# A decoder layer on one core: gated columns moved ahead of the second latent columns, and 38 convolution taps shared by ScalarE and GpSimd

## The chip, the core and the metric

The kernel runs on one core of a Trainium2 chip. The time is the device time of one execution, in microseconds (us). The core's engines work side by side, each through a queue of its own in order: TensorE (PE in the profile; PEld is its weight load), VectorE (DVE), ScalarE (ACT), GpSimd (POOL) and SyncE (SP), which here issues nearly all DMAs. They wait for each other through semaphores.

## What is computed

One step of a one-layer decoder with two parallel groups, for a prompt of 512 rows and 64 sample rows (8 sequences of 8), cut from the reference:

```python
proj = h @ w_in                                   # h = rmsnorm(x): 1024 -> 384 + 256 + 32 + 2*512
cq, ckv, kr, glu_in = ...                         # the 672 latent columns, the 1024 gated ones
q = einsum('btc,chd->bthd', rmsnorm(cq, g_q_norm), w_uq)
kv_rows = concat([rmsnorm(ckv, g_kv_norm), rope(kr)])
glu = glu_in[..., :512] * sigmoid(glu_in[..., 512:])
o_lat = attention over kv_rows (prompt), over 2048 cached rows + kv_rows (sample)
y = causal depthwise conv of glu, width 31, + b_dw          # 31 taps for each of 512 channels
conv_y = silu(layernorm(y, g_ln, b_ln))
x = x + concat([rmsnorm(attn), rmsnorm(conv_y)]) @ w_o
x = x + gated MLP with a width-3 convolution              # 1024 -> 2*2816 -> 1024
```

## The kernel before

Rows are kept transposed: channels lie on the 128 partitions, the 512 prompt and 64 sample rows along the free axis. Every matmul is made three times, with each operand split in a high and a low part (`mm3`, `mm3x`); `split` makes the parts, ScalarE the high one (CAST, L110) and VectorE the low one (L111). The stages are:

1. Input norm, transposed into `hTh`/`hTl`.
2. `latent_cols(0)`: the first 336 latent columns, PSUM banks named `pq`.
3. `glu()`: a generator over four blocks m of 128 gated channels. A block is two steps, the sigmoid half first, each of 48 matmuls of 288 columns into two banks `gb`, with weights `wg` from `wload`. After the second, VectorE writes `gx[:, m]` (L291 to L293), the input of the convolution. Weight tiles, raw, high and low, have two buffers each, so the high part of a step can be cast only when the matmuls of the step two before are done. The five banks of the stage go round, so a bank that `gx` reads is wanted again three steps later.
4. `latent_cols(1)`: the other 336 latent columns, three chunks of weights `w`, 45, 45 and 30 matmuls.
5. `latent(i)`, `q_rows`, `sample_queries`: norms, rotary parts and queries. Each `latent(i)` has GpSimd compute a reciprocal root (`rstd_of`, L119).
6. Sample attention in slots J = 0 to 37, four to a sequence, over key chunks of 512 rows: transposes `ktb`, scores `sb`, probabilities `ptb`, values `ob`.
7. `conv_norm`: from slot `CN0` on, two half steps a slot: transposes of the convolution's result `acc` (`lnb`), its statistics, `lnt`, the silu.
8. Prompt attention, output projection, gated MLP (`up`, `down`): the 600 us behind.

The convolution needs 31 taps for each of the four blocks m; a tap multiplies 128x512 elements of `gx[:, m]`, shifted by k, by a column of weights and adds the product to `acc[:, m]`. VectorE does a tap in one instruction (L246, SCALAR_TENSOR_TENSOR); GpSimd needs two, a product into a tile `ct` of two buffers (L249, TENSOR_SCALAR) and a sum (L250, TENSOR_TENSOR). `conv_sample(m)` is the same for the sample rows, on VectorE: per half a product `cs` of 128x992 (L258) and a sum (L260).

Before, four GLU steps (`GL0`) come first: block 0 and block 1. VectorE does taps 0 to 19 of block 0, GpSimd the other 11 into `acc2`; then `latent_cols(1)`, one GLU step, and three more between the queries. GpSimd does all 31 taps of block 1 and, behind the last `latent`'s reciprocal root (`issue_after(last["pow"])`), all of block 3 and four of block 2; VectorE does 12 taps of block 2 ahead of the slots and 15 more, one a slot, between them (`later`). `conv_norm` starts in slot 21.

What sets the order: the kernel is written for a scheduler, which puts each engine's instructions in one fixed sequence by their dependences and a running priority. `with prio(key)` shifts that priority for a block (a positive number: later). On the chip each engine then takes its sequence in order.

Of the kernel before, what the change touches and what calls it, by code (L numbers as in the profile page):

```python
# [10 lines left out]
F32 = mybir.dt.float32  # L11
# [3 lines left out]
AF = mybir.ActivationFunctionType  # L15
ALU = mybir.AluOpType
# [3 lines left out]
P = 128  # L20
NP = 512
# [42 lines left out]
def hymba_step(ctx, tc, x, cache, pt, sconv, sffn, vec, rows, w1, wglu, wuq, wuk, wuv, wukT,  # L64
# [79 lines left out]

    # ------------------------------------------------------------------ pools, first loads
    PR = dict(p0=-20, pr=-30, fs=-60, expo=80, wv=140, ft=-40, f0=-600, v2=600, av=-75, cs0=600, cv=65, vs=-55, cn=-150, att=-80, cs1=600, l4=20, q0=305, later=80, h2=70, l1=50, sq0=-45, lo=-360, wk=80, vb=20, lT=-15, v0=40, gl2=70, wo=-540, g0=-600, rq=600, cso=600, gl1=-40, sc1=25, rr=80, keys=-35, k0=600, pn=15, fs0=-60, ho=-45)

# [34 lines left out]
    def vcol(key, i):  # L182
        a = VEC[key][0] + i
        return vc[:, a:a + 1]
# [23 lines left out]

    # ------------------------------------------------------------------ input norm
    hTh = ps0.tile([P, 8, NT], F32R, name="hTh")  # L210
    hTl = ps0.tile([P, 8, NT], F32R, name="hTl")
    for i, (t0, n) in enumerate(TILES):
# [6 lines left out]
        for g in range(2):  # L219
# [5 lines left out]

    # ------------------------------------------------------------------ GLU columns, depthwise convolution
    GP = CW - 1 + NP
# [6 lines left out]
           for k in range(8)]  # L234
    acc = pcv.tile([P, 4, NT], F32, name="acc", tag="acc")

    def conv_taps(m, ks, E, first, dst=None):
        am = acc[:, m, 0:NP] if dst is None else dst
        for j, k in enumerate(ks):
            w = vcol("wdw", m * CW + k)  # L240
            xm = gx[:, m, k:k + NP]
            if j == 0 and first:
                b = vcol("bdw", m) if dst is None else 1.0
                E.tensor_scalar(am, xm, w, b, ALU.mult, ALU.add if dst is None else ALU.mult)
            elif E is V:
                V.scalar_tensor_tensor(am, xm, w, am, ALU.mult, ALU.add)  # L246
            else:
                t = pql.tile([P, NP], F32, name="ct", tag="ct", bufs=2)
                G.tensor_scalar(t, xm, w, 1.0, ALU.mult, ALU.mult)  # L249
                G.tensor_tensor(am, am, t, ALU.add)  # L250

    def conv_sample(m, E):
# [10 lines left out]

    GL0 = 4
    NV0 = 20
    NV2 = 12
    NV3 = 0
    NG2 = 4
    NL = 1
    LA = 0  # L270
    LS = 2
    last["kl"] = {}
    acc2 = pcv.tile([P, NP], F32, name="acc2")

# [35 lines left out]
    pj.append(ps1.tile([P, 672], F32, name="pj4", tag="pj4"))  # L310
    def latent_cols(c, order):
        pb = [bank("pq") for _ in range(5)]
        for (k0, kn) in ((0, 3), (3, 3), (6, 2)):
            w = wload(wp, w1[c][:, k0 * 336:(k0 + kn) * 336], kn * 336, "w1")
            for i in order:
                t0, n = TILES[i]
                for k in range(kn):
                    sl = slice(k * 336, (k + 1) * 336)
                    mm3(pb[i][:n, :336], hTh[:, k0 + k, t0:t0 + n], hTl[:, k0 + k, t0:t0 + n],
                        w[0][:, sl], w[1][:, sl], k0 + k == 0, k0 + k == 7)  # L320
        for i in order:
            n = TILES[i][1]
            A.copy(pj[i][:n, c * 336:(c + 1) * 336], pb[i][:n, :336])
# [5 lines left out]
    gl = glu()  # L329
    for _ in range(GL0):  # L330
        next(gl)
    with prio("cs0"):
        conv_sample(0, V)
    with prio("v0"):
        conv_taps(0, range(NV0), V, True)
    with prio("g0"):
        conv_taps(0, range(NV0, CW), G, True, acc2)
    latent_cols(1, ORD)

# [113 lines left out]
    with prio("l4"):  # L453
        latent(4)
        split(krn[:DR, 0], krn[:DR, 1], krT[:, NP:NT])
    with prio("gl1"):
        next(gl)
    wq_ = [wload(wp, wuq[c], 1152, "wuq") for c in range(2)]
# [6 lines left out]
    for i in range(4):  # L465
# [10 lines left out]
        with prio("rq"):  # L476
            rope_rows(qv[:, :, DN:], qv[:, :, DN:], i, P, H, "rq")
    with prio("cs1"):
        conv_sample(1, V)
    with tc.issue_after(last["pow"]):  # L480
        conv_taps(1, range(CW), G, True)
    for _ in range(4):
        with prio("sq1"):
            next(sq_, None)
        with prio("gl2"):
            next(gl, None)
    for _ in gl:
        pass

# [6 lines left out]

    with prio("v2"):
        conv_taps(2, range(NV2), V, True)
    V.tensor_tensor(acc[:, 0, :NP], acc[:, 0, :NP], acc2, ALU.add)

    def wload_into(hi, lo, src):
# [3 lines left out]

    later = [(2, -1)] + [(2, k) for k in range(NV2, CW - NG2)] + [(3, -1)] + [(3, k) for k in range(CW - NV3, CW)]
    with tc.issue_after(last["pow"]):
        conv_taps(3, range(CW - NV3), G, True)
        if NG2:
            conv_taps(2, range(CW - NG2, CW), G, True, acc2)  # L510

    s1.close()

    # ------------------------------------------------------------------ sample attention
    use_banks(k="k", s="s", x="x", o="o", b="k")
# [12 lines left out]
    RAW = 2  # L528
    CN0 = 21
    page_dma = []  # L530
# [251 lines left out]

    # ------------------------------------------------------------------ prompt attention
    R = {}
# [16 lines left out]
    def open_left():  # L801
# [171 lines left out]

    # ------------------------------------------------------------------ order of work
    assert NV2 > 0 and len(later) <= NL * (CN0 - LS)
    for J in range(NCR):
# [7 lines left out]
    for J in range(NJ + 6):  # L984
        if J == NJ + 1:
            open_right()
        if J == CN0 and NG2:
            G.tensor_tensor(acc[:, 2, :NP], acc[:, 2, :NP], acc2, ALU.add)
        if J >= CN0:
# [6 lines left out]
        if J == 30:  # L996
            wv = pcv.tile([P, 2, 1024], F32R, name="wv", tag="gx")
            with prio("wv"):
                wload_into(wv[:, 0], wv[:, 1], wuv)
        for m, k in later[:NL if J >= LS else 0]:  # L1000
            later.pop(0)
            with prio("later"), tc.issue_after(last["kl"][J + LA]):
                if k < 0:
                    conv_sample(m, V)
                else:
                    conv_taps(m, [k], V, False)
        if J >= CN0:
# [352 lines left out]
```

## Time and profile before

| | |
|---|---|
| three runs | 921.27 us median, 921.2 to 922.46 |
| profiled execution: span from first to last instruction | 919.5 us |
| around the span, taken as median less span | 1.8 us |
| PE busy | 864.1 us, 94% |
| mean granted TensorE clock | 0.976 |
| chain that ended last | PE 72%, POOL 18%, DVE 5% |

The profile gives no time of the profiled execution beyond its span; the difference to the median is taken as the work around it. A row of a timeline reads: start, duration, engine, line, operation, what it writes and reads, tile shapes, the count of instructions that stand together, and in brackets the engine's idle time before it and what ended that. Line numbers in rows are those of the kernel before.

### The profile page before, as it was taken

How to read it: one execution, taken by the hardware profiler on the slowest of the kernel's cores; microseconds unless marked ns; L12 is line 12 of the kernel's file. 1: busy time of each engine (PE TensorE's matmuls, PEld its weight loads, DVE VectorE, ACT ScalarE, POOL GpSimd, SP SyncE). 2: the span in 40 equal slices, each digit the busy share in tenths (PEclk: the TensorE clock that was granted, in tenths of full speed). 3: DMA queues.
4: the chain of work that ended last, by engine and by line, in shares of the span. 5: the costliest groups of instructions: out<-in, count | busy, mean ns of one | idle time of the engine just before them, and what ended most of it. 6: DMA issues, size and time to landing. Idle time of an engine off the chain costs nothing.

```text
span 919.5 us, 15985 instructions
## 1 busy us (share of the span) xinstructions
PE 864.1 (94%) x5820; PEld 773.8 (84%) x5820; DVE 606.3 (66%) x1097; ACT 431.4 (47%) x1008; POOL 288.3 (31%) x378
## 2 busy tenths in 40 slices
PE   7997977799989999998989999999999999999995
PEld 5997867666667767876769999999999999999995
DVE  6289789899987677777675666673124667665333
ACT  6322633577758976455453334333223343333333
POOL 3076299999981110000111122110001112211222
PEclk9998989899999999999999999999999999999998
DMA  7222114454442014011233222222332223223212
GB/s 231 81 61 75 58 62 130 123 153 117 116 110 80 26 47 149 24 47 28 65 109 115 91 89 73 86 64 67 88 110 94 75 87 92 71 63 99 70 41 104
DMA packets 37651, 79.80 MB, mean 87 GB/s; under 512 B 4226, under 2 KB 21699, under 8 KB 37572
## 3 DMA queue, kind: packets, MB, share of 16 engines
q1 hardware_dynamic: 37282, 78.22, 28.2%
q8 instruction: 46, 0.75, 0.3%
q10 hardware_dynamic: 290, 0.56, 0.2%
q14 instruction: 33, 0.27, 0.1%
HBM read 74.78 MB, written 3.98 MB: 86 GB/s over the span
## 4 chain that ended last, share of the span: by engine, by line
PE 72%; POOL 18%; DVE 5%; issue 2%; ACT 2%; DMA 1%; POOLq 0%; DVEq 0%; ACTq 0%
PE ub L129 10%; PE ub L131 10%; PE ub L133 10%; POOL acc L250 10%; POOL ct L249 7%; PE db L133 5%; PE db L131 5%; PE db L129 5%; PE ob L651 2%; PE wob L123 2%; PE wob L125 2%; PE wob L124 2%; DVE acc L246 2%; PE pq L125 1%; PE pq L124 1%
## 5 line engine op out<-in xcount | busy, mean ns | idle before, releaser
L129 PE MATMUL ub<-h2h,wup_h 128*128 128x288 f32 x704 | 154.0, 296 | 0.0
L131 PE MATMUL ub<-h2l,wup_h 128*128 128x288 f32 x704 | 153.9, 295 | 0.0
L133 PE MATMUL ub<-h2h,wup_l 128*128 128x288 f32 x704 | 152.7, 294 | 0.0
L133 PEld LDWEIGHTS ub<-h2h,wup_l 128*128 128x128 f32 x704 | 114.4, 189 | 0.0
L129 PEld LDWEIGHTS ub<-h2h,wup_h 128*128 128x128 f32 x704 | 114.0, 189 | 0.2
L131 PEld LDWEIGHTS ub<-h2l,wup_h 128*128 128x128 f32 x704 | 114.2, 189 | 0.0
L111 DVE TENSOR_TENSOR wup_l<-wup_r,wup_h 128x1024 fp32r<-128x1024 f32 x44 | 53.9, 1225 | 84.0 <-ACT wup_h L110 84.0
L250 POOL TENSOR_TENSOR acc<-acc,ct 128x512 f32<-128x512 f32 x73 | 108.1, 1480 | 2.8
L1180 POOL COPY nf<-U 128x2 f32<-128x2 f32 x44 | 28.7, 652 | 216.5 <-ACT U L1178 216.5
L249 POOL TENSOR_SCALAR ct<-gx,vc 128x512 f32<-128x512 f32 x73 | 78.8, 1090 | 0.0
L119 POOL TENSOR_TENSOR rstd<-ms,mhalf 128x1 f32<-128x1 f32 (+3 forms) x25 | 17.1, 687 | 195.5 <-ACT junk L971 111.4
L131 PE MATMUL db<-gl,wdn_h 128*128 128x288 f32 x352 | 78.4, 297 | 0.0
L129 PE MATMUL db<-gh,wdn_h 128*128 128x288 f32 x352 | 78.1, 299 | 0.0
L133 PE MATMUL db<-gh,wdn_l 128*128 128x288 f32 x352 | 77.6, 297 | 0.0
L110 ACT CAST wup_h<-wup_r 128x1024 fp32r<-128x1024 f32 x44 | 46.2, 1051 | 41.3 <-PE ub L131 30.7
L111 DVE TENSOR_TENSOR wdn_l<-wdn_r,wdn_h 128x768 fp32r<-128x768 f32 (+1 forms) x32 | 28.4, 888 | 54.9 <-ACT wdn_h L110 54.9
L110 ACT CAST wdn_h<-wdn_r 128x768 fp32r<-128x768 f32 (+1 forms) x32 | 25.0, 781 | 74.7 <-PE db L131 64.2
L131 PEld LDWEIGHTS db<-gl,wdn_h 128*128 128x128 f32 x352 | 57.9, 190 | 0.0
L133 PEld LDWEIGHTS db<-gh,wdn_l 128*128 128x128 f32 x352 | 57.5, 190 | 0.0
L129 PEld LDWEIGHTS db<-gh,wdn_h 128*128 128x128 f32 x352 | 57.0, 189 | 0.0
L246 DVE SCALAR_TENSOR_TENSOR acc<-gx,vc,acc 128x512 f32<-128x512 f32 x45 | 54.2, 1204 | 0.8
L110 ACT CAST gh<-uo 128x512 fp32r<-128x512 f32 (+1 forms) x44 | 16.9, 431 | 77.8 <-DVE uo L1191 77.8
(352 smaller groups left out, 2096.6 us busy)
## 6 DMA issues: line engine op xcount, KB each, us to landing
wup_r<-in_wup_dram SPq DMA_DIRECT2D x44, 512.0 KB, 3.5
CR<-in_cache_dram SPq DMA_DIRECT2D x128, 144.0 KB, 2.2
wdn_r<-in_wdn_dram SPq DMA_DIRECT2D x16, 384.0 KB, 3.1
wdn_r<-in_wdn_dram SPq DMA_DIRECT2D x16, 320.0 KB, 2.9
x<-in_x_dram SPq DMA_DIRECT2D x8, 512.0 KB, 5.9
wg_r<-in_wglu_dram SPq DMA_DIRECT2D x8, 512.0 KB, 3.2
wo_r<-in_wo_dram SPq DMA_DIRECT2D x8, 512.0 KB, 3.5
out_y_dram<-x SPq DMA_DIRECT2D x4, 512.0 KB, 3.2
```

Of the source, the lines that this page charges most:

```text
L110: A.copy(hi, src)
L111: last["split"] = V.tensor_tensor(lo, src, f(hi), ALU.subtract).ins
L123: T.matmul(out, lh, rh, start=start, stop=False)
L124: T.matmul(out, lh, rl, start=False, stop=False)
L125: T.matmul(out, ll, rh, start=False, stop=stop)
L129: T.matmul(o, lh, rh, start=start, stop=False)
L131: T.matmul(o, lh, rl, start=False, stop=False)
L133: T.matmul(o, ll, rh, start=False, stop=stop)
L246: V.scalar_tensor_tensor(am, xm, w, am, ALU.mult, ALU.add)
L249: G.tensor_scalar(t, xm, w, 1.0, ALU.mult, ALU.mult)
L250: G.tensor_tensor(am, am, t, ALU.add)
L1180: G.tensor_copy(nf[:, ch, 0:2], u[:, NP:UP])
```

## The change

All eight GLU steps follow `latent_cols(0)` directly (`GL0 = 8`). Of block 0, VectorE takes taps 0 to 23; the other 7 and all 31 of block 1 are shared: ScalarE multiplies a shifted piece of `gx` by its weights (`A.activation` with `scale=w`) into `ct`, GpSimd adds it. These 38 are traced four after each GLU step from the third on and one after each row tile of `latent_cols(1)`, and are kept in that order on both engines. GpSimd does blocks 2 and 3 alone, 62 taps, behind the last latent's reciprocal root. The four `conv_sample` run in slots 4, 8, 12 and 16, and `conv_norm` starts in slot 23.

```diff
+    acc2 = ps1.tile([P, NP], F32, name="acc2")
+    def shared_taps():
+        for m, am, ks in ((0, acc2, range(NV0, CW)), (1, acc[:, 1, 0:NP], range(CW))):
+            for k in ks:
+                w = vcol("wdw", m * CW + k)
+                xm = gx[:, m, k:k + NP]
+                if k == ks[0]:
+                    b = vcol("bdw", m) if k == 0 else 0.0
+                    tc.keep_in_program_order(A.activation(am, xm, AF.Identity, scale=w, bias=b))
+                else:
+                    t = pql.tile([P, NP], F32, name="ct", tag="ct", bufs=2)
+                    tc.keep_in_program_order(A.activation(t, xm, AF.Copy, scale=w))
+                    tc.keep_in_program_order(G.tensor_tensor(am, am, t, ALU.add))
+                yield
-    GL0 = 4
-    NV0 = 20
-    NV2 = 12
...
+    GL0 = 8
+    NV0 = 24
...
-    for _ in range(GL0):
+    for t in range(GL0):
         next(gl)
-    with prio("cs0"):
-        conv_sample(0, V)
+        if t > 1:
+            taps(4)
     with prio("v0"):
-        conv_taps(0, range(NV0), V, True)
-    with prio("g0"):
-        conv_taps(0, range(NV0, CW), G, True, acc2)
-    latent_cols(1, ORD)
+        first_taps()
+    latent_cols(1, ORD, 1)
+    taps(2 * CW)
+    V.tensor_tensor(acc[:, 0, :NP], acc[:, 0, :NP], acc2, ALU.add)
...
-    with prio("cs1"):
-        conv_sample(1, V)
-    with tc.issue_after(last["pow"]):
-        conv_taps(1, range(CW), G, True)
...
-    with prio("v2"):
-        conv_taps(2, range(NV2), V, True)
...
     with tc.issue_after(last["pow"]):
-        conv_taps(3, range(CW - NV3), G, True)
-        if NG2:
-            conv_taps(2, range(CW - NG2, CW), G, True, acc2)
+        conv_taps(2, range(CW))
+        conv_taps(3, range(CW))
...
-    CN0 = 21
+    CN0 = 23
...
-        for m, k in later[:NL if J >= LS else 0]:
-            later.pop(0)
+        for m in [J // 4 - 1] if J % 4 == 0 and 4 <= J < 20 else ():
             with prio("later"), tc.issue_after(last["kl"][J + LA]):
-                if k < 0:
-                    conv_sample(m, V)
-                else:
-                    conv_taps(m, [k], V, False)
+                conv_sample(m, V)
```

What the scheduler makes of it. VectorE in the gated stage, from the fourth weight split on; L245 and L247 are VectorE's taps now, L318 to L320 write `gx`. Of the change:

```order
L111 TENSOR_TENSOR wg_l<-wg_r,wg_h 128x1024
L245 TENSOR_SCALAR acc<-gx,vc 128x512
L247 SCALAR_TENSOR_TENSOR acc<-gx,vc,acc 128x512 x7
L111 TENSOR_TENSOR wg_l<-wg_r,wg_h 128x1024
L247 SCALAR_TENSOR_TENSOR acc<-gx,vc,acc 128x512 x5
L318 TENSOR_TENSOR gx<-gb,sg 128x288
L319 TENSOR_TENSOR gx<-gb,sg 128x224
L320 TENSOR_TENSOR gx<-gb,sg 128x8x8
L111 TENSOR_TENSOR wg_l<-wg_r,wg_h 128x1024
L247 SCALAR_TENSOR_TENSOR acc<-gx,vc,acc 128x512 x7
L111 TENSOR_TENSOR wg_l<-wg_r,wg_h 128x1024
L247 SCALAR_TENSOR_TENSOR acc<-gx,vc,acc 128x512 x4
```

The splits of the fifth, sixth and seventh GLU step stand behind runs of 7, 5 and 7 taps; before, no such split stood behind a run of taps until the fifth step, which came after `latent_cols(1)`.

ScalarE in the same stage, from the sigmoid of block 1 on; L270 and L273 are the scaled taps, L316 the sigmoid. Of the change:

```order
L316 ACTIVATE sg<-gb 128x288 x2
L270 ACTIVATE acc_252<-gx,vc 128x512
L273 ACTIVATE ct<-gx,vc 128x512 x6
L110 CAST wg_h<-wg_r 128x1024
L270 ACTIVATE acc<-gx,vc 128x512
L110 CAST wg_h<-wg_r 128x1024
L316 ACTIVATE sg<-gb 128x288 x2
L273 ACTIVATE ct<-gx,vc 128x512 x8
L110 CAST wg_h<-wg_r 128x1024
L110 CAST w_h<-w_r 128x1008
L316 ACTIVATE sg<-gb 128x288 x2
L273 ACTIVATE ct<-gx,vc 128x512 x8
```

Behind it follow the cast of the second chunk, 10 `ct`, the cast of the third chunk, 4 `ct`, the cast of the first `wuq` and then the copies of the latent rows. Before, only casts and sigmoids stood there.

TensorE where `conv_norm` begins (`lnb`); `pnb` is the one small transpose of a sequence's new probabilities, the fifth in both programs. Before:

```order
L107 MATMUL ktb<-ident,CR 128x128 x8
L585 MATMUL sb<-kh,QL 128x512
L586 MATMUL sb<-kl,QL 128x512
L107 MATMUL ptb<-ident,S 128x64
L107 MATMUL lnb<-ident,acc 128x128 x4
L107 MATMUL ptb<-ident,S 128x64 x7
```

Of the change:

```order
L663 MATMUL ob<-cl,PT 64x256
L665 MATMUL ob<-CR,PF 64x256 x2
L107 MATMUL ktb<-ident,CR 128x128 x7
L107 MATMUL pnb<-ident,S 64x64
L107 MATMUL lnb<-ident,acc 128x128 x4
L107 MATMUL ktb<-ident,CR 128x128
```

The first `lnb` moves from the start of slot 21 to behind the fifth `pnb`, at the end of slot 22.

## Rows read from the trace of the kernel before

**Rows 1.** The page: the chain that ended last, shares of the span by engine.

```profile
PE 72%; POOL 18%; DVE 5%; issue 2%; ACT 2%; DMA 1%; POOLq 0%; DVEq 0%; ACTq 0%
```

**Rows 2.** The chain in order of time, 105 to 116 us and 266 to 300 us: start, us, what.

```profile
110.72 0.69 POOL rstd L119
111.42 1.13 POOL acc L244
...
271.97 1.36 POOL acc L988
273.81 0.74 PE ptb L107 x7
```

**Rows 3.** TensorE's waits, 50 to 300 us: us in total, times, longest us.

```profile
PE sb L586 <- DVE kl L111: 6.7, 1, 6.7
PE pq L124 <- DVE w_l L111: 5.2, 2, 4.2
...
PE lnb L107 <- POOL acc L988: 2.6, 1, 2.6
```

**Rows 4.** Timeline of TensorE where the convolution's norm begins.

```profile
273.38 0.44 PE L107 MATMUL lnb<-ident,acc 128*128 128x128 f32 x2 [2.63 <-POOL acc L988]
...
280.06 0.66 PE L107 MATMUL lnb<-ident,acc 128*128 128x128 f32 x4
...
285.56 0.24 PE L107 MATMUL pnb<-ident,S 64*64 64x64 f32 x1
```

**Rows 5.** Windows: us, busy us of PE, PEld, DVE, ACT, POOL; PEclk, DMA share, GB/s.

```profile
273.40:285.80 12.40, 12.40 (x69) 8.60 (x70) 9.23 (x26) 7.46 (x17) 1.50 (x2) 0.86 0.21 60
```

**Rows 6.** Timeline of VectorE: splits and taps beside GpSimd's sums and beside none.

```profile
51.43 1.23 DVE L111 TENSOR_TENSOR wg_l<-wg_r,wg_h 128x1024 fp32r<-128x1024 f32 x1
...
70.26 2.30 DVE L111 TENSOR_TENSOR w_l<-w_r,w_h 128x1008 fp32r<-128x1008 f32 x1
...
74.79 1.67 DVE L246 SCALAR_TENSOR_TENSOR acc<-gx,vc,acc 128x512 f32<-128x512 f32 x1
...
84.56 0.75 DVE L246 SCALAR_TENSOR_TENSOR acc<-gx,vc,acc 128x512 f32<-128x512 f32 x1
```

**Rows 7.** Timeline of GpSimd: two sums beside VectorE's taps, two beside light work.

```profile
74.19 3.42 POOL L250 TENSOR_TENSOR acc<-acc,ct 128x512 f32<-128x512 f32 x2
...
167.80 2.64 POOL L250 TENSOR_TENSOR acc<-acc,ct 128x512 f32<-128x512 f32 x2
```

**Rows 8.** Timeline of ScalarE: sigmoid, copy of latent tile 4, a pass over 128x512.

```profile
57.69 0.70 ACT L289 ACTIVATE sg<-gb 128x288 f32<-128x288 f32 x2
...
85.62 0.43 ACT L323 COPY pj<-pq 64x336 f32<-64x336 f32 x1 [4.92 <-PE pq L125]
...
153.97 0.62 ACT L637 CAST ch<-CR 128x512 fp32r<-128x512 f32 x1 [5.37 <-PE gb L131]
```

**Rows 9.** Windows of TensorE alone: the four GLU steps of before.

```profile
37.63:63.30 25.67, 25.67 (x195) 1.00 0.24 74
```

**Rows 10.** Timeline of TensorE around its wait for the third latent chunk.

```profile
79.30 0.31 PE L125 MATMUL pq<-w_h,hTl 128*128 128x336 f32 x1
79.45 0.32 PE L123 MATMUL pq<-w_h,hTh 128*64 128x336 f32 x1
83.92 0.54 PE L124 MATMUL pq<-w_l,hTh 128*64 128x336 f32 x1 [4.15 <-DVE w_l L111]
...
88.74 0.48 PE L123 MATMUL pq<-w_h,hTh 128*128 128x336 f32 x1
89.02 0.48 PE L124 MATMUL pq<-w_l,hTh 128*128 128x336 f32 x1
```

**Rows 11.** GpSimd's groups by form, 163.4 to 189.8 us: count, busy us, mean ns.

```profile
L250 POOL TENSOR_TENSOR acc<-acc,ct 128x512 f32<-128x512 f32 x12 | 16.6, 1386 | 0.4
L249 POOL TENSOR_SCALAR ct<-gx,vc 128x512 f32<-128x512 f32 x11 | 9.7, 893 | 0.0
```

**Rows 12.** Windows of GpSimd's sums alone (line 250), its last stretch: us, busy us.

```profile
227.50:270.60 43.10, 26.07 (x18) 1.00 0.42 114
```

More of the change, by code (lines that the diff above doesn't have):

```diff
@@ L143, in wload @@
         return hi, lo
-    PR = dict(p0=-20, pr=-30, fs=-60, expo=80, wv=140, ft=-40, f0=-600, v2=600, av=-75, cs0=600, cv=65, vs=-55, cn=-150, att=-80, cs1=600, l4=20, q0=305, later=80, h2=70, l1=50, sq0=-45, lo=-360, wk=80, vb=20, lT=-15, v0=40, gl2=70, wo=-540, g0=-600, rq=600, cso=600, gl1=-40, sc1=25, rr=80, keys=-35, k0=600, pn=15, fs0=-60, ho=-45)
+    PR = dict(ca=0, p0=-20, pr=-30, fs=-60, expo=80, wv=140, ft=-40, f0=-600, v2=600, av=-75, cs0=600, cv=65, vs=-55, cn=-150, att=-80, cs1=600, l4=20, q0=305, later=80, h2=70, l1=50, sq0=-45, lo=-360, wk=80, vb=20, lT=-15, v0=40, gl2=70, wo=-540, g0=-600, rq=600, cso=600, gl1=-40, sc1=25, rr=80, keys=-35, k0=600, pn=15, fs0=-60, ho=-45)
     class prio:
@@ L235, in hymba_step, with first_taps, conv_taps @@
     acc = pcv.tile([P, 4, NT], F32, name="acc", tag="acc")
-    def conv_taps(m, ks, E, first, dst=None):
-        am = acc[:, m, 0:NP] if dst is None else dst
-        for j, k in enumerate(ks):
+    acc2 = ps1.tile([P, NP], F32, name="acc2")
+    def first_taps():
+        am = acc[:, 0, 0:NP]
+        for k in range(NV0):
+            w = vcol("wdw", k)
+            xm = gx[:, 0, k:k + NP]
+            if k == 0:
+                V.tensor_scalar(am, xm, w, vcol("bdw", 0), ALU.mult, ALU.add)
+            else:
+                V.scalar_tensor_tensor(am, xm, w, am, ALU.mult, ALU.add)
+    def conv_taps(m, ks):
+        am = acc[:, m, 0:NP]
+        for k in ks:
             w = vcol("wdw", m * CW + k)
             xm = gx[:, m, k:k + NP]
[L242 to L246, printed above, removed]
+            if k == 0:
+                G.tensor_scalar(am, xm, w, vcol("bdw", m), ALU.mult, ALU.add)
             else:
@@ L250, in conv_taps, with taps @@
                 G.tensor_tensor(am, am, t, ALU.add)
+    def shared_taps():
+        for m, am, ks in ((0, acc2, range(NV0, CW)), (1, acc[:, 1, 0:NP], range(CW))):
+            for k in ks:
+                w = vcol("wdw", m * CW + k)
[3 more added lines that the diff above has]
+                    tc.keep_in_program_order(A.activation(am, xm, AF.Identity, scale=w, bias=b))
+                else:
+                    t = pql.tile([P, NP], F32, name="ct", tag="ct", bufs=2)
+                    tc.keep_in_program_order(A.activation(t, xm, AF.Copy, scale=w))
+                    tc.keep_in_program_order(G.tensor_tensor(am, am, t, ALU.add))
+                yield
+    st_ = shared_taps()
+    def taps(n):
+        for _ in range(n):
+            next(st_, None)
     def conv_sample(m, E):
@@ L262, in conv_sample @@
         V.tensor_scalar(acc[:, m, NP:], acc[:, m, NP:], vcol("bdw", m), None, ALU.add)
-    GL0 = 4
-    NV0 = 20
-    NV2 = 12
-    NV3 = 0
-    NG2 = 4
+    GL0 = 8
+    NV0 = 24
     NL = 1
@@ L272, in hymba_step @@
     last["kl"] = {}
-    acc2 = pcv.tile([P, NP], F32, name="acc2")
     c0 = CW - 1
@@ L310, in hymba_step, with latent_cols @@
     pj.append(ps1.tile([P, 672], F32, name="pj4", tag="pj4"))
-    def latent_cols(c, order):
+    def latent_cols(c, order, nt=0):
         pb = [bank("pq") for _ in range(5)]
@@ L320, in latent_cols @@
                         w[0][:, sl], w[1][:, sl], k0 + k == 0, k0 + k == 7)
+                taps(nt)
         for i in order:
@@ L455, in hymba_step @@
         split(krn[:DR, 0], krn[:DR, 1], krT[:, NP:NT])
-    with prio("gl1"):
-        next(gl)
+    next(gl, None)
     wq_ = [wload(wp, wuq[c], 1152, "wuq") for c in range(2)]
@@ L484, in hymba_step @@
             next(sq_, None)
[L485 to L488, printed above, removed]
     def conv_state(g):
@@ L495, in conv_state @@
         nc.scalar.dma_start(oconv[:, 2 * g:2 * g + 2], cso)
-    with prio("v2"):
-        conv_taps(2, range(NV2), V, True)
-    V.tensor_tensor(acc[:, 0, :NP], acc[:, 0, :NP], acc2, ALU.add)
     def wload_into(hi, lo, src):
@@ L504, in wload_into @@
         split(hi, lo, raw)
-    later = [(2, -1)] + [(2, k) for k in range(NV2, CW - NG2)] + [(3, -1)] + [(3, k) for k in range(CW - NV3, CW)]
+    later = range(4)
     with tc.issue_after(last["pow"]):
-        conv_taps(3, range(CW - NV3), G, True)
-        if NG2:
-            conv_taps(2, range(CW - NG2, CW), G, True, acc2)
+        conv_taps(2, range(CW))
+        conv_taps(3, range(CW))
     s1.close()
@@ L972, in head_ss @@
                          accum_out=ssa[:, i, p_:p_ + 1])
-    assert NV2 > 0 and len(later) <= NL * (CN0 - LS)
     for J in range(NCR):
@@ L986, in hymba_step @@
             open_right()
-        if J == CN0 and NG2:
-            G.tensor_tensor(acc[:, 2, :NP], acc[:, 2, :NP], acc2, ALU.add)
         if J >= CN0:
```

## The prediction

> **What bounds the kernel now.** Read the shares of the chain that ended last first: TensorE holds 72%, GpSimd 18% [rows 1]. Then the same chain in order of time: GpSimd enters it at 110.7 us with the last latent's reciprocal root, stays on it through all taps that it starts at 111.4, and gives it back at 273.3 [rows 2]. So for 162 us the chain is GpSimd's list of taps, and TensorE's waits show where it bites: 2.6 us before `lnb`, the first transposes of the convolution's result [rows 3]. Before 165 us TensorE waits mostly for VectorE: 6.7 us for the first keys' low part, 4.2 for the third latent chunk [rows 3]. Behind `lnb` TensorE is busy without a gap [rows 5], so whatever moves that release moves the end.
>
> Two things therefore decide: when GpSimd ends its taps, and how much other TensorE work is done by then. A difference of 0.2%, 1.84 us, is about what a measurement of this kernel can tell from none.
>
> **How much later the release may come.** The first `lnb` moves from slot 21 to just behind the fifth `pnb`. In the trace these lie at 273.4 and 285.6, 12.2 us apart [rows 4]. Of that 1.8 is convolution norm, which stays behind `lnb` (half of the first `lnb`, a second one and as long a transpose back: 0.44 + 0.66 + 0.66) [rows 4]. The granted clock there is 0.86 [rows 5], partly on the lower of its two levels (1.2 against 2.4 GHz) after the 2.6 us of idling; 0.14 of 12.4 is 1.7 us at most, of which I take 1.5, for not all that runs there is bound by the clock. A TensorE that waits for `lnb` again pays that again. So a release at 273.4 + 12.2 - 1.8 - 1.5 = **282.3** gives the same end.
>
> **The gated stage, which is longer now.** TensorE's four GLU steps took 25.67, 6.4 each [rows 9]; eight from 37.6 on would end at 88.8. They won't.
> - Prices. A VectorE tap takes 0.75 alone and 1.67 beside GpSimd's sums; a split of some 1000 columns 1.23 alone and 2.30 beside sums [rows 6]. Two sums take 2.64, 1.32 each, beside light work and 3.42, 1.71 each, beside taps [rows 7]. A scaled tap on ScalarE isn't in the trace. Nearest rows: half a sigmoid of 288 columns from PSUM, 0.35, below; a cast of 128x512 from SBUF, 0.62, above [rows 8]; I take 0.62, the same size from the same memory. It counts only where GpSimd waits for the first of a run.
> - GpSimd has nothing to do until ScalarE has done block 1's sigmoid, at 58.4 [rows 8], and two passes of 0.62: first sum at 59.7. Until then VectorE does its first 8 taps undisturbed and splits the fifth step's weights at 60.1. Its next 5 stand beside sums: 5 x 1.7 (0.03 between) to 68.6, then `gx` (0.9) and the sixth split to 70.7; TensorE wants that 0.5 after 69.6 and loses 0.6.
> - Then 7 taps, 2 alone and 5 beside sums that begin at 72.2, to 80.8, and the seventh split at 2.3 to 83.1. TensorE wants it at 77.1: **6.0 lost**. The wait for the third chunk before shows what follows: matmuls start 0.155 apart ahead of 4.15 us of idling and 0.28 apart behind it, still at 89.0 [rows 10]. That is the lower clock; I take 2 us. The seventh step ends at 91.0.
> - ScalarE queues the first chunk's cast (its buffer is read by that step) and block 3's sigmoid ahead of 8 scaled taps, so sum 15 of 36 starts only at 93.5. The other 22, mostly 1.37 with their gap, a third of them beside splits, at 1.43: to 125.
> - The third chunk's cast stands behind 10 scaled taps, and the last of those waits for sum 30, at 116.3: high part 117.6, low part 119.2. TensorE is through chunk 2 at 112.5 (91.0, a step of 6.4, 1.0 until VectorE's last `gx` frees its bank, 90 matmuls at 0.155) and loses **6.7**, and 2.6 more on the lower clock. That it is TensorE's loss changes little: behind 4 more scaled taps and the cast of `wuq` (1.2) tile 4's copy ends at 123.9.
> - Before, that copy started at 85.6 [rows 8] and GpSimd's taps at 111.4 [rows 2]: 25.8, in which TensorE also did one GLU step, 6.4. Without it, and with less of it on the lower clock: 18.5. **GpSimd begins its 62 taps at 142.4**, 31 later than before.
>
> **What is saved.** The last three gated steps no longer stand between the queries, nor 12 taps ahead of the keys, behind which `sb` waited 6.7 us [rows 3]. By these same steps the first scores come about when they came before, 163 us: the stalls move ahead, they don't add up. VectorE loses 23 taps, gains no others; four sample convolutions in slots replace two, at 6 to 7 us each, so the slots win little and TensorE would reach `lnb` near 280. ScalarE's 38 passes, 24 us, fill a stage in which it was mostly idle, and their cost is the order of its queue, counted above. The four gated steps' DMAs on SP are the same, only earlier. Convolution norm's 18 half steps from slot 23 on end in slot 32, before anything wants them; starting two slots later costs nothing of its own.
>
> **The tap pace.** GpSimd before did 66 taps and one sum in 162 us. Now it has 62, with VectorE's taps gone. Nearest rows: 163 to 190 us, with three VectorE taps and one sample convolution, 1.386 + 0.893 = 2.28 [rows 11]; above, the last stretch: 18 sums in 43.1 us, 17.5 taps, 2.46 [rows 12]; below, 1.32 [rows 7] and half of it for a product, 2.0. I take 2.28, since one sample convolution in four slots is about that stretch's load: 62 x 2.28 = 141.4, and the end at **283.8**.
>
> **The sum.** 283.8 against 282.3 is +1.5. On the profiled execution: 919.5 + 1.5, and 1.8 around the span, which is also its distance to the median; 921.27 + 1.5, taken down a little because the queries lose VectorE's splits too, gives **922.5**: no difference that can be told, at the slow edge of it. Its own range, 3 us on the start and 3 on the pace: 918 to 927.
>
> **Rivals.**
> - **Faster: the gated stage flows.** If taps and sums disturb each other only in part, as where VectorE's mean over its early taps counts (1.2), the seventh split comes 4 earlier, sums run at 1.37, and the 62 taps start at 137. End 278.4, TensorE itself ready at about 275: 3.9 under the mark, **917**. For: before, TensorE lost as much ahead of 165 us, so there is room. Against: 1.67 and 1.71 are what stands beside each other [rows 6, 7], and sums without products between leave no gap. 0.33.
> - **Slower: the slots slow GpSimd.** Four sample convolutions among VectorE's steady work hold the pace near the last stretch's 2.46 [rows 12]. At 2.37, halfway, 62 taps end at 289.3: 7 over, **928**; at 2.46, 934. It decides from 2.29 on, which ends at 284.4, 2.1 over the mark. For: those products `cs` now fall in every fourth slot. Against: that stretch held four VectorE taps as well. 0.18.
> - **Slower: a full block.** Rows 6 and 7 add up to 0.75 + 1.32 = 2.07 if a tap and a sum took turns, against 1.7 beside each other. Taking turns, some ten pairs on the way to the seventh split and the second run cost 0.37 each: 3.5 later, **926**. The Trainium skill (SBUF — State Buffer, "SBUF: two separate sides") has VectorE and GpSimd hold their shared port pair for a whole instruction, so that "the other fully blocks"; the trace agrees that they slow each other, at 1.7 and not 2.07. 0.05.
> - **The change doesn't do what it says: not shared, but in turn.** Were each scaled tap to wait for the sum before it, 22 sums would cost 0.62 more each: start 156, **936**. Two `ct` buffers speak against it. 0.04.
>
> **How the numbers follow.** Forecast 0.40, of which 0.06 lies faster than 0.2%, 0.16 within, 0.18 slower; the rival above 0.33, nearly all faster; the three slower ones 0.27, mostly slower, though a short delay may end within the bound. Together faster 0.37, same 0.21, slower 0.42. For 8 in 10 the range takes in the flowing stage with 3 us to spare, 914, and the slots at 2.37 with 2 more, 930.
>
> **What would show it.** Right: `gb` waiting 6 us for `wg_l` near 77, `pq` as long for `w_l` near 113; first tap of block 2 near 142; taps at 2.28; `lnb` waiting for GpSimd's last sum at 284. Wrong: no wait of the gated stage over 3 us, or the first tap before 138; or a release that TensorE doesn't wait for, and then the slots' work sets the end.

## The result, and the profile after

The changed kernel takes **928.38 us** (median of 7 runs, 924.81 to 928.85) against 922.13 for the kernel before (7 runs, 921.2 to 924.54): ratio **1.0063, 95% interval 1.0049 to 1.0078**. It is slower by 6 us, over three times what can be told. The profiled execution has a span of 926.6 us, 7.1 more than before, at a mean granted clock of 0.965.

The page's chain that ended last, which answers [rows 1]:

```profile
PE 76%; DVE 8%; ACT 4%; POOL 4%; issue 3%; SPq 2%; DMA 1%; POOLq 0%; DVEq 0%; ACTq 0%
```

GpSimd fell from 18% to 4%: its list of taps is off the chain. TensorE's waits from 50 to 300 us, beside [rows 3]:

```profile
PE gb L133 <- DVE wg_l L111: 6.1, 1, 6.1
PE pq L123 <- ACT w_h L110: 5.1, 1, 5.1
PE krb L107 <- ACT RP L564: 4.8, 1, 4.8
```

The first two were forecast, the third was not, and no `lnb` is among them. GpSimd's timeline (the 15th to 36th shared sum; the first of its 62 taps, behind the last latent's reciprocal root; the last two sums):

```profile
92.86 31.24 POOL L274 TENSOR_TENSOR acc<-acc,ct 128x512 f32<-128x512 f32 x22 [7.46 <-ACT ct L273]
...
142.70 1.13 POOL L256 TENSOR_SCALAR acc<-gx,vc 128x512 f32<-128x512 f32 x1
...
282.59 3.15 POOL L260 TENSOR_TENSOR acc<-acc,ct 128x512 f32<-128x512 f32 x2
```

and TensorE's, from the first scores to the convolution's norm, which answers [rows 4]:

```profile
162.67 0.79 PE L599 MATMUL sb<-kh,QL 128*128 128x512 f32 x1 [0.46 <-ACT kh L110]
163.90 0.80 PE L600 MATMUL sb<-kl,QL 128*128 128x512 f32 x1 [0.43 <-DVE kl L111]
...
170.38 0.47 PE L107 MATMUL krb<-ident,RP 128*128 128x128 f32 x1 [4.83 <-ACT RP L564]
...
203.90 0.24 PE L107 MATMUL pnb<-ident,S 64*64 64x64 f32 x1
...
287.98 0.24 PE L107 MATMUL pnb<-ident,S 64*64 64x64 f32 x1
288.15 0.66 PE L107 MATMUL lnb<-ident,acc 128*128 128x128 f32 x4
```

GpSimd's last sum ends at 285.74; TensorE gets to `lnb` at 288.15 and waits for nothing. The release was ready 2.4 us before anyone wanted it. So the question is why TensorE was at the fifth `pnb` only at 288, where [rows 4] has it at 285.6 with 2.6 us of waiting and 1.8 of norm in it. (`pnb`, the small transpose of a sequence's new probabilities, is the same work in both programs, and so a fixed point for comparing them.)

**Where the new wait comes from.** `krb` transposes `RP`, the rotary columns of four chunks of cached rows, which ScalarE copies out of the buffers `CR`. ScalarE, after, the second to fourth copy:

```profile
165.33 0.30 ACT L564 COPY RP<-CR 128x128 f32<-128x128 f32 x1 [2.22 <-DMA CR<-in_cache_dram]
...
167.93 0.30 ACT L564 COPY RP<-CR 128x128 f32<-128x128 f32 x1 [1.79 <-DMA CR<-in_cache_dram]
170.03 0.30 ACT L564 COPY RP<-CR 128x128 f32<-128x128 f32 x1 [1.79 <-DMA CR<-in_cache_dram]
```

All three wait for their loads; the first copy, at 161.0, did not. SP's queue, after (four loads to a chunk; the second row is cut at 163 by its window, and the loads go on):

```profile
154.63 1.94 SPq L557 DMA_DIRECT2D CR<-in_cache_dram  x4
...
160.92 2.39 SPq L557 DMA_DIRECT2D CR<-in_cache_dram  x5
```

and before:

```profile
135.93 36.25 SPq L543 DMA_DIRECT2D CR<-in_cache_dram  x30
```

Before, the first loads went out at 135.9; now the second chunk's go out at 160.9. VectorE tells why. After and then before, the last rotary part of the queries, which `rope_rows` writes from a scratch tile:

```profile
160.18 0.72 DVE L379 TENSOR_TENSOR qtok<-rq,rq 128x256 f32<-128x256 f32 x1
```

```profile
132.61 0.40 DVE L351 TENSOR_TENSOR qtok<-rq,rq 128x256 f32<-128x256 f32 x1
```

The load follows the end of that instruction by 0.02 us. The slots' pools take over the queries' memory, and the second chunk's buffer lies where the scratch tile lay. Before, the queries' ropes ended at 133.0 and TensorE still had gated steps between the queries to do until 154, over which the loads came in. With all gated steps done early, the queries are the last thing before the slots, and the loads stand behind them in the open. TensorE's 40 us around it (columns as in [rows 5]), after and then before:

```profile
160.00:200.00 40.00, 31.36 (x145) 23.96 (x145) 26.94 (x47) 24.05 (x50) 39.30 (x38) 0.68 0.55 153
```

```profile
160.00:200.00 40.00, 32.77 (x172) 24.00 (x172) 34.38 (x62) 25.22 (x56) 39.38 (x36) 0.85 0.47 126
```

The trace has 27 matmuls fewer in these 40 us, at a granted clock of 0.68 against 0.85. The first scores' low part is 1.0 us later than before (163.90 against 162.87, the end of the wait of 6.7 in [rows 3]); the first `pnb`, at 203.90 against 196.38, is 7.5 later. From there to the fifth it is 84.1 us now and 89.2 before; less the 2.6 of waiting, the 1.8 of norm and the prediction's 1.5 for the clock, that was 83.3. So nearly all that is lost ahead of `lnb` is lost between the first scores and the first `pnb`.

**And behind `lnb`.** From the fifth `pnb` to the end it is 638.6 us now and 633.9 before, 4.7 more. 1.8 of this is the norm that stood ahead of it. The rest is as much as TensorE's waits there come to, 288.5 to 365 us:

```profile
PE ptb L107 <- ACT S L621: 1.8, 2, 1.3
PE sb L599 <- DVE mx L606: 0.7, 1, 0.7
PE lns L107 <- DVE PT L111: 0.4, 1, 0.4
```

2.9 in all, against 0.2 before over the same work (286 to 358 us).

### The profile page after: what moved, and what is told of

The parts are those of the page before. It is cut to its first block, busy times and chain, and to the rows that moved or that the text cites. A ratio compares the mean times of both kernels' runs of the same rounds, so it can differ in the third digit from the quotient of the medians.

```text
span 926.6 us, 16047 instructions
## 1 busy us (share of the span) xinstructions
PE 868.1 (94%) x5820; PEld 778.2 (84%) x5820; DVE 579.7 (63%) x1074; ACT 457.4 (49%) x1046; POOL 291.6 (31%) x385
## 4 chain that ended last, share of the span: by engine, by line
PE 76%; DVE 8%; ACT 4%; POOL 4%; issue 3%; SPq 2%; DMA 1%; POOLq 0%; DVEq 0%; ACTq 0%
PE ub L129 10%; PE ub L133 10%; PE ub L131 10%; PE db L131 5%; PE db L133 5%; PE db L129 5%; POOL acc L274 4%; PE ktb L107 3%; PE ob L665 2%; PE wob L123 2%; PE wob L125 2%; PE wob L124 2%; DMA CR<-in_cache_dram 1%; PE sb L599 1%; PE tb L107 1%
## 5 line engine op out<-in xcount | busy, mean ns | idle before, releaser
L111 DVE TENSOR_TENSOR wup_l<-wup_r,wup_h 128x1024 fp32r<-128x1024 f32 x44 | 53.9, 1225 | 84.1 <-ACT wup_h L110 84.1
L260 POOL TENSOR_TENSOR acc<-acc,ct 128x512 f32<-128x512 f32 x60 | 84.9, 1415 | 2.3
L274 POOL TENSOR_TENSOR acc<-acc,ct 128x512 f32<-128x512 f32 x36 | 53.5, 1485 | 50.3 <-ACT ct L273 47.7
L111 DVE TENSOR_TENSOR kl<-ktb,kh 128x512 fp32r<-128x512 f32 x64 | 42.9, 683 | 22.1 <-ACT kh L110 21.8
L259 POOL TENSOR_SCALAR ct<-gx,vc 128x512 f32<-128x512 f32 x60 | 55.3, 934 | 0.0
```

Of the source, the lines that this page charges most:

```text
L111: last["split"] = V.tensor_tensor(lo, src, f(hi), ALU.subtract).ins
L274: tc.keep_in_program_order(G.tensor_tensor(am, am, t, ALU.add))
```

## The experiments

Theory A: the cached rows arrive late, since their loads stand behind the queries' last rope and no gated step covers them. Rivals: B, the work of VectorE and ScalarE in the slots sets the pace; C, GpSimd's release decides after all; D, sharing the taps is what costs. Each run stands beside runs of the kernel before on its chip (medians 921.3 to 921.7).

**`pages`**: the first four chunks in the other pool.

```diff
-        late = J % NCR in range(4, 8)
+        late = J % NCR in range(0, 4)
```

> Edit: the buffers of the first four chunks of cached rows lie in the pool on the right, those of the second four in the pool on the left; nothing else. Theory A (cached rows late): in the changed kernel 12 of the first 16 page loads go out only at 160.9 us, behind VectorE's last rotary part of the queries, because their buffers lie on the queries' memory; ScalarE's copy of the rotary columns waits for them and TensorE idles 4.8 us before the first krb. Moved off that memory the loads go out right behind the last output of the latent rows, near 150, that wait falls under 1 us, TensorE is 4 to 6 us earlier in the first slots, and lnb is then held by GpSimd's last sum near 285.7; time 2 to 5 us lower than the changed kernel (923.5 to 926.5). Rival B (VectorE's work in the slots sets the pace): the wait only moves into the next slots, lnb stays at 287 to 289, time within 1 us of the changed kernel.

936.82 us, 1.0164 [1.0151, 1.0178]: 8 above the change, the opposite of what A expected. The other pool lies over the queries' weights, and SP waited 9.9 us for their last split:

```profile
162.93 0.91 SPq L557 DMA_DIRECT2D CR<-in_cache_dram  x2
```

The loads came later still. From 346 us on it also has another order of work, in the prompt's attention (644.1 from the fifth `pnb` to the end), so its time tells little.

**`nosamp`**: no sample convolution in the slots, zeros in its columns.

```diff
-        for m in [J // 4 - 1] if J % 4 == 0 and 4 <= J < 20 else ():
+        for m in [J // 4 - 1] if J % 4 == 0 and 4 <= J < 4 else ():
```

> Edit: the four sample convolutions in slots 4, 8, 12 and 16 are left out (zeros stand in the sample columns); the rest is as in the changed kernel. Theory A: the wait for the rotary columns before the first krb (4.8 us) stays; GpSimd's taps go at 2.15 to 2.2 instead of 2.31 and end 7 us earlier, but TensorE wasn't waiting for them, so only the short waits for the probabilities in slots near the samples go, 1 to 2.5 us. Rival B (the samples on VectorE slow the slots): lnb 4 to 7 us earlier and the time 4 us or more lower. Rival C (GpSimd's release still decides): the time follows the release, 7 us lower.

925.93 us, 1.0044 [1.003, 1.0058]. GpSimd, then TensorE:

```profile
270.86 2.98 POOL L261 TENSOR_TENSOR acc<-acc,ct 128x512 f32<-128x512 f32 x2
```

```profile
171.26 0.47 PE L107 MATMUL krb<-ident,RP 128*128 128x128 f32 x1 [4.93 <-ACT RP L565]
...
287.13 0.63 PE L107 MATMUL lnb<-ident,acc 128*128 128x128 f32 x4 [0.48 <-DVE PT L111]
```

GpSimd ends at 273.8, 12 us earlier, and `lnb` comes 1.0 earlier: this rules out C. The wait ahead of `krb` stays. The time is 2.4 us below the change's, with intervals that overlap; that is what A allowed, and short of the 4 of B.

**`cn25`**: `CN0 = 25`.

> Edit: convolution norm starts in slot 25 instead of 23. Theory A: TensorE reached lnb 2.4 us behind GpSimd's last sum and waited for nothing there, so two slots later changes nothing: within 1 us of the changed kernel, unless the last steps of the norm now stand behind the last slot (then up to 2 us more). Rival C (the release decides): 2 to 3 us lower.

933.75 us, 1.013 [1.011, 1.015]. The fifth `pnb` is where it was (287.70), so up to there A held; the stretch behind it grew to 644.8, against 638.6 and, in the run `again` below, 641.0. The norm two slots later is no gain, which is against C, and costs 4 to 6 us in what follows. A had allowed 2: this part of its expectation missed.

**`gl8`**: the kernel before with all gated steps first, and nothing else.

```diff
-    GL0 = 4
+    GL0 = 8
...
-        next(gl)
+        next(gl, None)
```

> Edit: the kernel before with all eight gated steps directly behind the first latent columns, and nothing else of the change: GpSimd keeps 11 taps of block 0 and 66 others, VectorE its 47, no scaled taps. Theory A: the first 16 pages again wait for the last rotary part of the queries, TensorE idles 3 us or more for the rotary columns, and GpSimd, which starts block 1 only behind the last latent's root near 125 to 135 and needs 66 taps of 2.3 to 2.45, ends at 280 to 295, where conv norm in slot 21 waits for it: 925 to 940, slower than the kernel before by 4 or more. Rival D (the sharing of the taps is what costs): 915 to 921, faster than the kernel before.

937.25 us, 1.0172 [1.0158, 1.0186].

```profile
268.47 0.44 PE L107 MATMUL lnb<-ident,acc 128*128 128x128 f32 x2
286.73 0.69 PE L107 MATMUL lnb<-ident,acc 128*128 128x128 f32 x2 [17.82 <-POOL acc L988]
```

The gated steps first alone cost 16 us, nearly all of it in this wait: GpSimd ends at 286.7, 13.4 later than before, while TensorE was at `lnb` earlier (268.5 against 270.3). It also waited 4.1 us for `RP`, as A says. So D does not hold here: once the gated steps move, the rest of the change (the shared taps, the samples in the slots, the later norm) is needed, and gives back 9.

**`pages2`**: as `pages`, with the chunks over `hTh`, which nobody reads behind the second latent columns.

```diff
+    touch(pt_, ("S", [NS, KEYS], F32, 2), ("sl", [NS, 512], F32, 2))
```

> Edit: the buffers of the first four chunks of cached rows lie over hTh, whose last reader is the second latent columns, instead of over the queries' memory; every engine keeps the changed kernel's order through the sample slots. Theory A (cached rows late): the loads go out right behind the last output of latent rows, 150 to 159, the wait before the first krb falls from 4.8 us to under 1.5, the first new probabilities' transpose (pnb) comes 4 to 7 us earlier, at 197 to 200 instead of 203.9, and TensorE reaches lnb before GpSimd's last sum (285.7), so that only 2 to 4 us of it are kept: 923.5 to 926.5. Rival B (VectorE's and ScalarE's work in the slots sets the pace): pnb at 202 or later, lnb at 287 to 289, time within 1 us of the changed kernel.

933.47 us, 1.0144 [1.0123, 1.0165]. TensorE:

```profile
282.97 0.24 PE L107 MATMUL pnb<-ident,S 64*64 64x64 f32 x1
283.97 0.52 PE L107 MATMUL lnb<-ident,acc 128*128 128x128 f32 x3 [0.76 <-DVE PT L111]
284.82 0.33 PE L107 MATMUL lnb<-ident,acc 128*128 128x128 f32 x1 [0.33 <-POOL acc L260]
```

The wait ahead of `krb` is gone and the fifth `pnb` 5.0 us earlier, with GpSimd now the last to release `lnb`, as A has it. But the first `pnb`, which A put at 197 to 200, came at 202.5, where B had it: the queries took longer (first scores at 166.9 against 162.7, as in `again`). The time, 5 us above the change, is against both; from 340 us on the prompt's attention has another order, 646.1 from the fifth `pnb` to the end, so it does not answer the question.

**`pages2_cn22`**: the same with `CN0 = 22`.

> Edit: as in the run before, and convolution norm starts in slot 22 instead of 23. Theory A: TensorE waits 2 to 5 us for GpSimd's last sum at the first lnb, and the stretch behind the slots, which is 4 us longer in the changed kernel than before, gives back 1 to 3: within 2 us of the run before. Rival E (the norm's place, not the cached rows, cost the time behind the slots): 3 us or more below the run before.

938.06 us, 1.0182 [1.0165, 1.0199]: the first `lnb` waits 5.8 us for GpSimd, and the stretch behind the fifth `pnb` is 3.6 shorter than in `pages2`, part of which is norm done ahead. Neither expectation held.

**`share`**: the change with the gated steps as before, four first and four between the queries.

```diff
-    GL0 = 8
+    GL0 = 4
...
-    next(gl, None)
+    with prio("gl1"):
+        next(gl)
...
+        with prio("gl2"):
+            next(gl, None)
```

> Edit: the changed kernel with four gated steps ahead of the second latent columns and the other four between the queries, as in the kernel before; the sharing of the 38 taps, the 62 taps on GpSimd and the sample convolutions in the slots stay. Theory A: the gated steps cover the loads again, page loads go out near 136 to 150, no wait for the rotary columns, first scores at 158 to 162; GpSimd starts its 62 taps at 118 to 128 and ends at 260 to 272, ahead of slot 23: 914 to 921, 8 or more below the changed kernel. Rival D (the sharing itself costs, by holding casts on ScalarE and splits on VectorE): 924 or more.

937.32 us, 1.0174 [1.0157, 1.019]; A's forecast missed by 16. TensorE's waits, 50 to 300 us:

```profile
PE qb L123 <- ACT wuq_h L110: 9.2, 1, 9.2
PE pq L123 <- ACT w_h L110: 5.7, 1, 5.7
PE lnb L107 <- POOL acc L260: 5.4, 1, 5.4
```

With only four steps to hide in, the scaled taps hold up ScalarE's casts for the latent columns and the queries, as D says. But GpSimd shows a second cause:

```profile
154.59 0.77 POOL L256 TENSOR_SCALAR acc<-gx,vc 128x512 f32<-128x512 f32 x1 [21.76 <-DVE gx L319]
```

Its 62 taps begin with block 2, whose `gx` the sixth gated step, one of those between the queries, delivers only at 154. A had them start at 118 to 128; GpSimd stood idle for 21.8 us, ended at 293.0, and that is the wait ahead of `lnb`. Before, GpSimd had all of block 1 to do in the meantime. So D's time came, but the run does not test the sharing alone: it also starves GpSimd, and how the 16 us over the kernel before divide between the casts and the missing block stays open. What it does show is that the new division of the taps needs the gated steps early.

**`again`**: the changed kernel unaltered.

> The changed kernel itself, unaltered, beside the next two, since runs of some variants that keep its order differed by several us in the queries. Both theories: 927 to 930, a wait of about 4.8 us for the rotary columns ahead of the first krb, lnb near 288.

927.68 us (6 runs, 925.95 to 930.83), 1.0066 [1.005, 1.0081]. Time and `lnb` (288.22) are as expected; the wait ahead of `krb` missed, at 1.7 instead of 4.8, because the scores themselves came 5.5 us later, at 169.4 (last section).

**`rows_early`**: four tiles of the queries' pool change places, so that the scratch tile lies past the first four chunks. Every engine's order is the changed kernel's.

```diff
+    acc2 = ps1.tile([P, NP], F32, name="acc2")
+    gq = ps1.tile([P, DCQ], F32, name="gq")
+    gkv = ps1.tile([P, DC], F32, name="gkv")
+    rp = ps1.tile([P, 5, 2, 32], F32, name="rp")
     ones = ps1.tile([1, P], F32, name="ones", tag="rt1", bufs=2)
...
-    gq = ps1.tile([P, DCQ], F32, name="gq")
-    gkv = ps1.tile([P, DC], F32, name="gkv")
-    rp = ps1.tile([P, 5, 2, 32], F32, name="rp")
...
-    acc2 = ps1.tile([P, NP], F32, name="acc2")
```

> Edit: four small tiles of the queries' pool change places, so that VectorE's rotary scratch no longer lies under the buffer of the second chunk of cached rows; every engine keeps exactly the changed kernel's order, to the end. Theory A (cached rows late): the second to fourth chunk's loads go out at 156.7 to 163 instead of 160.9 to 166.8, the wait for the rotary columns falls from 4.8 us to 0.5 to 1.5, the first new probabilities' transpose (pnb) comes 3 to 6 us earlier, lnb at 284 to 286, where GpSimd's last sum (285.7) now stops it: 1.5 to 4 us below the changed kernel. Rival B (VectorE's and ScalarE's work in the slots sets the pace): the wait goes, but pnb and lnb come within 1 us of where they were, and so does the time.

**925.14 us** (5 runs, 924.46 to 926.03), 1.0043 [1.0029, 1.0056]: 2.5 below `again`, from the same chip. SP, GpSimd and TensorE:

```profile
156.84 1.94 SPq L557 DMA_DIRECT2D CR<-in_cache_dram  x4
```

```profile
282.24 2.61 POOL L260 TENSOR_TENSOR acc<-acc,ct 128x512 f32<-128x512 f32 x2
```

```profile
167.37 0.80 PE L600 MATMUL sb<-kl,QL 128*128 128x512 f32 x1
...
169.53 0.47 PE L107 MATMUL krb<-ident,RP 128*128 128x128 f32 x1 [0.51 <-ACT RP L564]
...
199.22 0.24 PE L107 MATMUL pnb<-ident,S 64*64 64x64 f32 x1
...
283.86 0.24 PE L107 MATMUL pnb<-ident,S 64*64 64x64 f32 x1
284.92 0.63 PE L107 MATMUL lnb<-ident,acc 128*128 128x128 f32 x4 [0.82 <-DVE PT L111]
```

The second chunk follows the first at once (the first waits for the queries' last matmul, 2 us later than expected), the wait ahead of `krb` is 0.5, the granted clock from 160 to 200 us is 0.83, the first `pnb` is 4.7 earlier than in the changed kernel's profile above and `lnb` 3.2, at GpSimd's release (284.85). Apart from the loads' own times expectation A held in every number; B's did not. This is the run that shows the late rows: by addresses alone, 2.5 us. The two intervals still touch, but of the 30 pairs of one run of each, 29 have `rows_early` faster. How the gain comes about is less plain than A has it: in this profile the first scores' low part comes 3.5 us later than in the changed kernel's (167.37 against 163.90), which by itself shortens the wait, so that `krb` is only 0.9 earlier. From there to the first `pnb` the same work takes 29.7 us instead of 33.5, at the higher granted clock.

**`rows_early_nosamp`**: the same without the sample convolutions.

> Edit: as in the run before, and the four sample convolutions in the slots are left out (zeros in the sample columns), so that GpSimd's last sum comes near 274 and cannot stop lnb. Theory A: lnb at 281 to 284, and the time 3 to 6 us below the changed kernel, 1 to 4 below the run that only leaves the sample convolutions out (925.9). Rival B: no more than 1 us below that run.

924.28 us, 1.0036 [1.0023, 1.0049]. TensorE:

```profile
166.05 0.47 PE L107 MATMUL krb<-ident,RP 128*128 128x128 f32 x1 [0.93 <-ACT RP L565]
```

Beside `nosamp` this is the cleaner pair of profiles: the first scores' low parts are 1.2 us apart (163.48 and 164.68), the wait falls from 4.9 to 0.9, and `krb` is 5.2 earlier, the first `pnb` 4.9 (199.79 against 204.69) and `lnb`, at 282.2, 4.9. What `krb` gains arrives at `lnb` nearly in full. The time is 1.7 lower, and the intervals overlap.

**`taps_behind`**: `rows_early` with `latent_cols(1, ORD, 0)`.

> Edit: the run rows_early, and no scaled taps among the second latent columns: 14 of them follow only behind the copies of the latent rows, so that ScalarE's cast of the third chunk no longer stands behind ten of them. Theory F (what is left over the kernel before is TensorE's waiting behind scaled taps): the wait for the third chunk (5.1 us) falls under 1, the queries begin 4 to 6 us earlier, and so do the first scores: 920 to 923. Rival G (GpSimd's queue only moves it): the 14 sums now stand between the second and the third latent's reciprocal roots, the queries wait there for as long, and the time is within 1.5 us of rows_early (925.1) or above it.

932.91 us, 1.0141 [1.0125, 1.0157]. GpSimd, and TensorE's longest wait:

```profile
115.53 0.81 POOL L119 TENSOR_TENSOR rstd<-ms,mhalf 128x2 f32<-128x2 f32 x1 [1.80 <-DVE ms L117]
116.31 20.11 POOL L274 TENSOR_TENSOR acc<-acc,ct 128x512 f32<-128x512 f32 x14
138.43 0.82 POOL L119 TENSOR_TENSOR rstd<-ms,mhalf 128x2 f32<-128x2 f32 x1 [2.01 <-DVE ms L117]
```

```profile
PE cqb L107 <- DVE pj L389: 12.7, 2, 9.9
```

G holds: 14 sums between two reciprocal roots cost more than the wait for the third chunk that they replace.

**`six_first`**: `rows_early` with `GL0 = 6` and the last two gated steps between the queries (the `next(gl)` lines of `share`).

> Edit: the run rows_early with six gated steps ahead of the second latent columns and two between the queries. Theory F: the wait for the seventh split (6.1 us) goes and two gated steps cover the queries' waits and the loads of cached rows: 917 to 922, at or under the kernel before. Rival G (as in the run with four steps first, where the queries' weights were cast late): the casts for the queries' weights stand behind scaled taps and TensorE waits for them, 926 to 936.

**920.95 us** (12 runs, 917.94 to 924.13), 0.9999 [0.9986, 1.0012]: what F expected, with no wait for casts of the queries' weights (G), and level with the kernel before, not ahead of it. TensorE:

```profile
163.43 0.50 PE L605 MATMUL sb<-kl,QL 128*128 128x512 f32 x1 [0.22 <-DVE kl L111]
...
164.36 0.27 PE L107 MATMUL krb<-ident,RP 128*128 128x128 f32 x1
...
194.08 0.24 PE L107 MATMUL pnb<-ident,S 64*64 64x64 f32 x1
...
280.31 0.24 PE L107 MATMUL pnb<-ident,S 64*64 64x64 f32 x1
280.49 0.66 PE L107 MATMUL lnb<-ident,acc 128*128 128x128 f32 x4
```

No wait ahead of `krb`, and the first `pnb` is 2.3 earlier than before. The first scores come when the changed kernel's do: the waits for the seventh split and the third chunk have given way to two others of `pq` (6.5 us for `w_l`, 6.2 for `gx`). So nearly the whole gain over the changed kernel, 9.8 us at the first `pnb`, lies behind the first scores. Block 2 is ready for GpSimd here, whose 62 taps start at 135.3 and end at 280.2. The stretch behind the fifth `pnb` is 640.5. Of all versions tried none beats the kernel before.

## Why the prediction came out small

928.4 lies in the range of 914 to 930, but the forecast was 922.5, no change that can be told, and it is 6 us slower. Its steps, with what the changed kernel's trace has (us):

| step | forecast | measured |
|---|---|---|
| first sum | 59.7 | 59.5 |
| wait for the seventh split, until | 6.0, 83.1 | 6.1, 82.6 |
| sum 15 starts, last sum ends | 93.5, 125 | 92.9, 124.1 |
| wait for the third chunk, high and low part | 6.7 | 5.1 + 1.5 |
| tile 4's copy ends | 123.9 | 123.5 |
| the 62 taps start, pace, end | 142.4, 2.28, 283.8 | 142.7, 2.31, 285.7 |
| first scores | 163 | 162.7, low part 163.9 |
| TensorE would reach `lnb` | near 280 | 288.2 |

- **The gated stage and GpSimd's list** were right, to 2 us at the far end. So "the gated stage flows" fell, with "in turn, not shared". The 62 taps start within 0.3 us of the forecast, and the pace taken from [rows 11] was 1% short.
- **"Slower: the slots slow GpSimd"** gave 928, which came, but for another reason: it needed a pace of 2.37 and a TensorE that waits for it. The pace was 2.31 and TensorE did not wait. That its time agrees is no evidence for it.
- **"A full block"** fell. VectorE's taps and GpSimd's sums beside each other, after:

```profile
71.96 5.07 DVE L247 SCALAR_TENSOR_TENSOR acc<-gx,vc,acc 128x512 f32<-128x512 f32 x3
```

```profile
71.68 13.71 POOL L274 TENSOR_TENSOR acc<-acc,ct 128x512 f32<-128x512 f32 x8 [1.10 <-ACT ct L273]
```

  A tap takes 1.69 and a sum 1.71, and they go one for one, where whole instructions in turn would make 2.07 a pair. The Trainium skill (SBUF — State Buffer, "SBUF: two separate sides") has the one that starts first hold the ports for the whole instruction, while "the other fully blocks"; taken at the recorded times, that is not what this trace shows.
- **The step that failed is in "What is saved"**: "The last three gated steps no longer stand between the queries" was booked as a saving, and "TensorE would reach `lnb` near 280" followed from equal first scores. That the scores come at 163 held. But the three steps were cover, some 20 us of TensorE's work between 130 and 154 us, for the queries' last ropes and for the cached rows, whose buffers those ropes hold. SP was looked at for the gated steps' own loads ("the same, only earlier") and not for what stands behind them in its queue. Booked at nothing, this leaves the forecast 8 us short at `lnb`. That addresses alone give back 3.2 at `lnb` and 2.5 of the time is shown by `rows_early`; that two steps back between the queries give back the remaining 4 is shown by `six_first`, which moves other waits as well.
- **The waiting is not all of it; the rest goes with the clock.** From the first scores' low part to the first `pnb` it is 40.0 us in the changed kernel at a granted clock of 0.68 from 160 to 200 us, 36.3 in `rows_early_nosamp` at 0.73, 31.9 in `rows_early` at 0.83, 30.7 in `six_first` at 0.91, and 33.5 before at 0.85. From 160 to 165 us, ahead of the wait for the rows, the clock is 1.00 in `six_first` and 0.50 in the changed kernel. Two pairs part the two. At nearly the same clock, `again` (36.9 at 0.66) waits 3.1 us less than the changed kernel's other profile and is 3.1 shorter; `rows_early_nosamp` waits 4.0 less than `nosamp` (40.0 at 0.67) and is 3.7 shorter. So a microsecond of waiting costs about one. What goes beyond that goes with the clock, which no run tests by itself, so how the 8 us divide is known only roughly.
- **Its own sign came.** Among the signs of being wrong stood "a release that TensorE doesn't wait for, and then the slots' work sets the end". TensorE did not wait, but `nosamp` leaves little for the slots' samples: what the start of the slots waits for set the end.
- **The mark** of 282.3 was a little late: `lnb` 5.9 us behind it came with a span 7.1 longer, 2.6 with 3.1, and in `six_first` 1.8 ahead of it with 1.3 longer. "Starting two slots later costs nothing of its own" does not hold: `cn25` shows that two slots later still is worse, and there are 2.9 us of waits behind `lnb` that were not there before. What makes these waits was not tested.
- The kernel before was not run with its loads held back, so A was tested on one side alone.

## What to carry to other kernels

Before booking work that leaves a stage as saved, ask what arrives under it: list the transfers that fall into that stage, and for each the instruction that frees its buffer. When one stage's memory is reused by the next, the last reader of a scratch tile can be what starts the next stage's first load, and moving one small tile, with every engine's order kept, gave back 2.5 of the 6 us here. Two parts of a change can each be bad alone and only halfway good together (16, 16 and 6 us here). Test them apart, but look in the trace at what the cut itself takes away: `share` lost time because one engine's list had lost its input, and not only by what it was meant to test.

## What the runs showed that was not expected

The same program in the same order does not run the queries alike. In the changed kernel's two profiles TensorE's stretch of 130 to 140 us had the full granted clock once, and 0.81, partly on the lower of its two levels (1.2 against 2.4 GHz), the other time (the profile of `again`):

```profile
130.00:140.00 10.00, 9.47 (x64) 7.78 (x64) 8.11 (x21) 6.87 (x24) 1.40 (x2) 1.00 0.17 56
```

```profile
130.00:140.00 10.00, 9.62 (x57) 7.72 (x57) 7.34 (x19) 5.75 (x19) 0.70 (x1) 0.81 0.17 56
```

From there the second falls back until its first scores' low part starts at 169.44 against 163.90, and VectorE's splits meet other instructions of GpSimd as well (the two splits of `wukT` took 1.21 and 1.43 beside GpSimd's products in one, 2.29 and 2.30 beside its sums in the other). And yet the fifth `pnb` comes at 287.98 and 288.05: the slots take up a delay of 5 us. Nothing here shows why the two executions differ. So a difference at the first scores is not yet a difference at the end, and one profile of each kernel would have put the cause in the wrong place.
